# Queries and keys of a hybrid mixer as one token-stationary block with seven-product pairs, and all scores ahead of the values

## The chip, the cores and the metric

The kernel runs on one core of one Trainium2 chip. The metric is the device time of one execution in microseconds (us). Engines are named as in the profile: PE is TensorE (PEld its weight loads), DVE is VectorE, ACT is ScalarE, POOL is GpSimd, SP is the engine whose queue issues nearly all DMAs.

## What is computed

One layer of a streaming encoder on 256 tokens of width 2048, in f32: a half-step feed-forward, a mixer, cross attention to 256 memory tokens, a second half-step feed-forward, a final norm. The change lies in the mixer (and in the last units of the feed-forward ahead of it):

```python
h = rms_norm(x, mix_norm)
proj = h @ w_in        # 2048 x 4112: pool 1024 | q 512 | k 512 | v 1024 | gate 1024 | low-rank decay 16
u, q, k, v, g, a_lr = jnp.split(proj, list(IN_SPLITS), axis=-1)
y_pool = pool_mixer(u, pool_w, pool_scale)       # 4 groups: trailing means over 2, 4, 8, 16 tokens, then 256 x 256 each
y_gla = gla_mixer(q, k, v, g, a_lr, gla_w_a2, gla_b_a, gla_head_norm)
x = x + jnp.concatenate([y_pool, y_gla], axis=-1) @ w_out
...
# in gla_mixer: 4 heads, key width 128, value width 256, chunks of 64 tokens
log_a = jax.nn.log_sigmoid(a_lr @ w_a2 + b_a) / 16
cum = jnp.cumsum(chunks(log_a, GLA_DK), axis=2)
k_dec = kc * jnp.exp(cum[:, :, -1:] - cum)
scores = einsum(qc, k_dec)       # also from each chunk to the chunks before it, with the decays between
o = scores @ v                   # then a norm per head, and the product with silu(g)
```

## The kernel before

**Products.** Every large product is made of units of 1 MB of weights, [128, 2048] per unit. A weight is split into a high part wh (ScalarE, L1585) and a low part wl (VectorE, L453, `low_parts`), and an activation likewise (xs for the normed input, ys for a stage's inner result, each [128, 16, 2, 256]: k-tile, high or low, token). A product is high by high, high by low and low by high. There are three kinds of block:

- `block_a` (weights stationary): per k-tile and 128 output columns one matmul of 512 columns (high weight by high and low activation) and one of 256 (low weight by high activation). The result has channels on the partitions and comes in two halves, which `joined` adds (ScalarE copies one half out of PSUM, VectorE adds). A unit has 16 such pairs of matmuls, a block of 512 output columns has four units.
- `block_b` and `block_t` (tokens stationary, `products` at L362): 24 matmuls of 512 columns per unit. The result has tokens on the partitions.
- `block_s` (tokens stationary, 1024 output columns, 8 units, one per pair of k-tiles): for some pairs, the "sevens", the four 128 x 512 block products are replaced by seven products of sums (`seven`, L507): 21 matmuls instead of 24. Such a unit needs sums of activation blocks (`Sums.make`, made once, VectorE and ScalarE) and sums of weight blocks (`split_seven`: three sums into a tile T, the raw blocks' parts xh and xl, the sums' parts wh and wl). Its parts take all four PSUM buffers from the first seven until `combine` after the last one; `join` then adds them to the ordinary products, once for each half.

**Order.** `Stream` holds a list of units and of small operations; `st.op(f, n)` puts an operation n units later. `emit` splits a unit's weights two units ahead of its products, and issues the load of a unit three further. wh and wl have three buffers each, the raw weights three. `in_turn`, `among_weights` and `behind_weights` fix the place of an operation among the weight splits of VectorE and ScalarE. Within these bounds a planner, which simulates the engines' times while the program is built, settles the order on each engine: an instruction that it does not take for ready is moved behind others. A tile with n buffers waits until the tile n allocations before it under the same name has been read for the last time. `shared_tile` lets T, xh and xl stand in other tiles' buffers, by the "homes" given to the scope.

**PSUM** has four buffers of [128, 2, 512].

**The mixer** (L940 to L1225) before: a block_a for each half of the pool columns (`ev_pool`, L971: trailing sums in three "m4" buffers, result into ys 8 to 15); the unit of the 16 decay columns (`a_unit`, L1035); `decay` (L1052); a block_a for the queries and one for the keys (`ev_q`, `ev_k`), with channels on the partitions as the scores need them; the pool unit (`pool_unit`, L1003: 48 matmuls of 256 columns, reads ys 8 to 15, writes ys 0 to 7); two block_b for the values, and among them the scores of each head (`scores`, L1130, its decayed query tile in one m4 buffer, one score tile "ST" for all heads) and the outputs (`attend`, L1156); two block_a for the gate. The normed input's last k-tiles (`fold`, L785) are made after the mixer's first unit; the norm's row factors come from `finish_norm`, and `spread_norm` turns them into a row over all partitions by a small matmul.

Of the kernel before, what the change touches and what calls it, by code (L numbers as in the profile page):

```python
# [9 lines left out]
AF = mybir.ActivationFunctionType  # L10
ALU = mybir.AluOpType
# [3 lines left out]
P = 128  # L15
D = 2048
# [83 lines left out]
def build(ctx, tc, I, out):  # L100
# [303 lines left out]
    class Sums:  # L404
# [1 line left out]

        def __init__(self, name, act, pairs, over, room):
            self.name, self.act, self.pairs, self.over = name, act, pairs, over  # L410
            self.room, self.where = room, {}

        def make(self, g):
            act, i = self.act, self.pairs.index(g)
            n = 3 if self.over else 4
            if i == 0 or i >= self.room:
                room, tag = (self.room, self.name) if i == 0 else (1, f"{self.name}{i}")
                t = scope["pool"].tile([P, room * 6 * P], F32R, tag=tag, name=uid(tag))
                held = min(len(self.pairs), self.room) if i == 0 else 1
                t = t[:, : held * 2 * n * P].rearrange("p (g a n s) -> p g a n s", a=2, n=n, s=P)  # L420
                self.where.update({i + k: t[:, k] for k in range(held)})
            own = self.where[i]
            a, k = jtile(), slice(2 * g, 2 * g + 2)
            nc.vector.tensor_tensor(
                out=a.rearrange("p (k s) -> p k s", k=2), in0=f32(act[:, k, 0, :]),
                in1=f32(act[:, k, 1, :]), op=ALU.add,
            )

            a = a.rearrange("p (n s) -> p n s", n=4)
            p11, p21, p12, p22 = (a[:, m] for m in range(4))  # L430
            nc.vector.tensor_tensor(out=p11, in0=p11, in1=p21, op=ALU.subtract)
            nc.vector.tensor_tensor(out=p21, in0=p22, in1=p21, op=ALU.subtract)
            nc.vector.scalar_tensor_tensor(
                out=p22, in0=p11, scalar=-1.0, in1=p22, op0=ALU.mult, op1=ALU.subtract
            )
            added = nc.vector.tensor_tensor(out=p12, in0=p12, in1=p22, op=ALU.add)
            split(own[:, 0], own[:, 1], a[:, 4 - n :])
            if self.over:
                split(act[:, 2 * g, 0, P:], act[:, 2 * g, 1, P:], p11)
            return None, added  # L440
# [377 lines left out]
    REST = IntoX((0,), (2,), ((1, 2, 3, 4, 0, 5), None), ((0,), ()), False)  # L818
    END = IntoX((0,), None, None, None)

    def into_x(w, act, scale, gain=None, k0=0, nk=KT, spread_too=True, src=None, way=OUTPUT):

        for b in range(2):
            st.op(lambda b=b: fetch_x(b, src), 2)
            cols = wwide(w, b * 2 * NB, k0, nk)
            if way.sevens[b]:
                block_s(cols, act, way.sums, way.orders[b], residual(scale, b, 0),
                        early_parts(scale, b), way.sevens[b])
            else:
                block_t(cols, act, residual(scale, b))  # L830
            if gain is not None:
                for j in range(2):
                    st.op(lambda c=2 * b + j: fold(c, gain), way.folds[2 * b + j])
        if gain is not None:
            st.op(lambda: finish_norm(4, spread_too), way.folds[3] + 1)
            if spread_too:
                st.op(spread_norm, 3)

    FF_PARTS = ((0, 4), (4, 4), (8, 3))

# [88 lines left out]
    st.op(more_gains, 14)  # L929
    st.op(lambda: turn_gains(G_MIX, G_END), 35)  # L930

    def down_first(wd, k0, nk, last, way):
        way.make_sums()
        into_x(wd, ys, 0.5, G_MIX if last else None, k0, nk, src=None if k0 else I["x"][0],
               way=way)

    ffn(I["ffn1_w_gate"][0], I["ffn1_w_up"][0], I["ffn1_w_down"][0], down_first,
        amid_first)
    st.op(close_scope, 1)
    st.op(open_scope("s_mix"), 1)  # L940


    w_in = I["w_in"][0]
# [7 lines left out]
    def mixer_constants():  # L951
        keep = mt("keep", [P, S])
        nc.gpsimd.memset(keep, 1.0)
        for c in range(S // CH):
            nc.gpsimd.memset(keep[:, c * CH : c * CH + 1], 0.0)
        wa2 = mt("wa2", [32, H * DK])
        for i in range(2):
            nc.sync.dma_start(wa2[16 * i : 16 * i + 16, :], I["gla_w_a2"][0])

    st.op(mixer_constants, 2)  # L960

# [90 lines left out]
    def decay():  # L1052
        v = four(ptile(uid("pz")))
        for h in range(H):
            nc.tensor.matmul(
                v[:, h, :], mix["wa2"][:, h * DK : (h + 1) * DK], mix["aT"], start=True, stop=True
            )
        z, e, cum = (as_four(m4()) for _ in range(3))
        for h in range(H):
            nc.scalar.activation(z[:, h, :], v[:, h, :], AF.Identity, bias=gcol(G_BA + h))  # L1060
        nc.scalar.activation(e, z, AF.Abs)
        nc.scalar.activation(e, e, AF.Exp, scale=-1.0)
        nc.scalar.activation(e, e, AF.Ln, bias=1.0)
        nc.vector.scalar_tensor_tensor(
            out=z, in0=z, scalar=0.0, in1=e, op0=ALU.min, op1=ALU.subtract
        )
        for h in range(H):
            nc.vector.tensor_tensor_scan(
                out=cum[:, h, :], data0=mix["keep"], data1=z[:, h, :], initial=0.0,
                op0=ALU.mult, op1=ALU.add,  # L1070
            )
        ends = cum.rearrange("p h (c t) -> p (h c) t", t=CH)[:, :, CH - 1 : CH]
        E = mt("E", [P, 4 * 4])
        nc.scalar.activation(E, ends.rearrange("p a b -> p (a b)"), AF.Exp, scale=1.0 / 16)
        nc.vector.tensor_tensor(
            out=e.rearrange("p h (c t) -> p (h c) t", t=CH),
            in0=ends.to_broadcast([P, 16, CH]),
            in1=cum.rearrange("p h (c t) -> p (h c) t", t=CH), op=ALU.subtract,
        )
        nc.scalar.activation(e, e, AF.Exp, scale=1.0 / 16)  # L1080
        nc.gpsimd.tensor_tensor(out=e, in0=e, in1=bc(rows["R"], H), op=ALU.mult)
        mix["e"] = e

        Ev = E.rearrange("p (h c) -> p h c", c=4)
        F = mt("F", [P, 3, 4])
        nc.vector.tensor_tensor(out=F[:, 0, :], in0=Ev[:, :, 1], in1=Ev[:, :, 2], op=ALU.mult)
        nc.vector.tensor_tensor(out=F[:, 1, :], in0=Ev[:, :, 2], in1=Ev[:, :, 3], op=ALU.mult)
        nc.vector.tensor_tensor(out=F[:, 2, :], in0=F[:, 0, :], in1=Ev[:, :, 3], op=ALU.mult)

    def ev_q(p, ps):  # L1090
        if p == 0:
            mt("q", [P, H, S])
        q = mix["q"][:, 2 * p : 2 * p + 2, :]
        joined(ps, q)
        nc.vector.scalar_tensor_tensor(
            out=q, in0=q, scalar=DK ** -0.5, in1=bc(rows["R"]), op0=ALU.mult, op1=ALU.mult
        )

    def ev_k(p, ps):
        if p == 0:  # L1100
            mt("k", [P, H, S])
        k = mix["k"][:, 2 * p : 2 * p + 2, :]
        joined(ps, k)
        nc.vector.tensor_tensor(out=k, in0=k, in1=mix["e"][:, 2 * p : 2 * p + 2, :], op=ALU.mult)

    block_a(wblock(w_in, 0), xs, ev_pool(0))
    block_a(wblock(w_in, NB), xs, ev_pool(1))
    st.unit(load_a, a_unit, split_a)
    st.op(ev_a)
    st.op(decay, 2)  # L1110
    block_a(wblock(w_in, 2 * NB), xs, ev_q)
    block_a(wblock(w_in, 3 * NB), xs, ev_k)
    st.unit(load_pool, pool_unit)
    for g in range(4):
        st.op(lambda g=g: pool_out(g))

    def ev_v(b):
        def evict(ps):
            if b == 0:
                mt("v", [P, 2, 2 * NB])  # L1120
                s = mt("ST", [P, 2, S])
                nc.gpsimd.memset(s[64:128, 0, 0:CH], 0.0)
                nc.gpsimd.memset(s[64:128, 1, 2 * CH : 3 * CH], 0.0)
            for h in range(2):
                nc.scalar.activation(
                    mix["v"][:, h, b * NB : (b + 1) * NB], ps[:, h, :], AF.Copy, scale=Rcol[:, h : h + 1]
                )
        return evict

    def scores(h):  # L1130
# [14 lines left out]
        for j in range(4):  # L1145
# [2 lines left out]
            nc.tensor.matmul(  # L1148
                ps[part, j // 2, j * CH : S], kd[:, j * CH : (j + 1) * CH], rhs, start=True, stop=True
            )  # L1150
        s = mix["ST"]
        for j in range(4):
            part = slice((j % 2) * CH, (j % 2 + 1) * CH)
            nc.vector.tensor_copy(s[part, j // 2, j * CH :], ps[part, j // 2, j * CH : S])

    def attend(h):  # L1156
        s, v = mix["ST"], mix["v"]
        po = ptile(uid("po"))
        for vt in range(2):
            col = h * DV + vt * P  # L1160
# [38 lines left out]
    def ev_g(b):  # L1199
# [10 lines left out]
            split_pair(ys, 8 + 2 * h, t)  # L1210
        return evict

    for b in range(2):
        block_b(wblock(w_in, (4 + b) * NB), xs, ev_v(b))
        for i in range(2):
            h = 2 * b + i
            at = 1 + i - b
            st.op(lambda h=h: scores(h), at)
            st.op(lambda h=h: attend(h), at + 1)
            st.op(lambda h=h: head_squares(h), at + 1)  # L1220
        st.op(lambda b=b: head_norms(b), 5 - 2 * b)
        st.op(lambda b=b: head_scale(b), 6 - b)
# [404 lines left out]
```

## Time and profile before

| | us |
|---|---|
| median of 3 runs (2080.21 to 2080.56) | 2080.51 |
| the profiled execution | 2080.73 |
| its span, first to last instruction | 2078.8 |
| TensorE busy in it | 2066.5 |
| VectorE busy | 1811.7 |
| ScalarE busy | 1148.4 |
| GpSimd busy | 98.7 |

Matmuls are pipelined: one of 512 columns is shown with 390 ns, while the next starts about 227 ns later. The pace is therefore read from the chain of waits, where a row gives the time from one matmul's end to the next, or from the starts in order of time. In rows of the timeline and of groups, what stands behind the arrow in brackets or after the bar is what ended the engine's idle time before the instruction. "pa" are results of block_a, "pb" of block_b, "pt" of block_t and block_s, "px" and "ph" transposes, "pq" scores, "po" outputs, "pp" the pool unit, "pz" the decay's small product.

### The profile page before, as it was taken

How to read it: one execution, taken by the hardware profiler on the slowest of the kernel's cores; microseconds unless marked ns; L12 is line 12 of the kernel's file. 1: busy time of each engine (PE TensorE's matmuls, PEld its weight loads, DVE VectorE, ACT ScalarE, POOL GpSimd, SP SyncE). 2: the span in 40 equal slices, each digit the busy share in tenths (PEclk: the TensorE clock that was granted, in tenths of full speed). 3: DMA queues.
4: the chain of work that ended last, by engine and by line, in shares of the span. 5: the costliest groups of instructions: out<-in, count | busy, mean ns of one | idle time of the engine just before them, and what ended most of it. 6: DMA issues, size and time to landing. Idle time of an engine off the chain costs nothing.

```text
span 2078.8 us, 24366 instructions
## 1 busy us (share of the span) xinstructions
PE 2066.5 (99%) x9645; PEld 1724.5 (83%) x9645; DVE 1811.7 (87%) x1708; ACT 1148.4 (55%) x1144; POOL 98.7 (5%) x87
## 2 busy tenths in 40 slices
PE   9999999999999999999999999999999999999998
PEld 7888888888888888888888888888888888888886
DVE  7998899989998677579889878889988999889987
ACT  7655455644555545456756554566554555545554
POOL 0000000000000000000000000000000010000001
PEclk9999999999999999999999999999999999999999
DMA  7666666566656755556755455666576665676664
GB/s 264 204 202 223 242 219 215 187 227 228 235 194 220 248 178 182 163 181 225 264 183 194 169 182 182 203 213 216 179 243 217 235 209 190 224 241 222 211 225 152
DMA packets 131179, 435.95 MB, mean 210 GB/s; under 512 B 9844, under 2 KB 13528, under 8 KB 130680
## 3 DMA queue, kind: packets, MB, share of 16 engines
q1 hardware_dynamic: 130888, 433.86, 61.9%
q8 instruction: 76, 1.25, 0.2%
q10 hardware_dynamic: 176, 0.53, 0.1%
q14 instruction: 39, 0.32, 0.0%
HBM read 417.58 MB, written 16.78 MB: 209 GB/s over the span
## 4 chain that ended last, share of the span: by engine, by line
PE 99%; DMA 0%; DVE 0%; ACT 0%; SPq 0%; issue 0%; DVEq 0%; ACTq 0%
PE pt L362 58%; PE pt L507 28%; PE pa L347 7%; PE pb L362 2%; PE ph L780 1%; PE pl L1321 1%; PE pv L1358 1%; PE px L791 1%; DMA x<-in_x 0%; PE pp L1012 0%; PE pe L362 0%; PE pa L1039 0%; PE po L1161 0%; PE tm L1268 0%; PE px L717 0%; PE pq L1148 0%
## 5 line engine op out<-in xcount | busy, mean ns | idle before, releaser
L362 PE MATMUL pt<-wh,xs 128*128 128x512 f32 x2080 | 667.6, 390 | 0.2 <-ACT xs L236 0.2
L453 DVE TENSOR_TENSOR wl<-raw,wh 128x2048 fp32r<-128x2048 f32 (+1 forms) x251 | 540.1, 2159 | 121.3 <-ACT wh L1585 120.9
L1585 ACT CAST wh<-raw 128x2048 fp32r<-128x2048 f32 x251 | 479.3, 1913 | 266.6 <-PE pt L362 110.7
L489 ACT CAST wh<-T 128x1024 fp32r<-128x1024 f32 x246 | 258.4, 1054 | 374.8 <-DVE T L486 362.7
L362 PEld LDWEIGHTS pt<-wh,xs 128*128 128x128 f32 x2080 | 389.8, 188 | 80.3 <-ACT xs L236 0.4
L362 PE MATMUL pt<-wh,ys 128*128 128x512 f32 x1440 | 454.7, 389 | 0.0
L362 PE MATMUL pt<-wl,xs 128*128 128x512 f32 x1040 | 405.5, 391 | 0.0
L362 PEld LDWEIGHTS pt<-wh,ys 128*128 128x128 f32 x1440 | 270.2, 188 | 55.7
L362 PE MATMUL pt<-wl,ys 128*128 128x512 f32 x720 | 280.7, 390 | 0.0
L453 DVE TENSOR_TENSOR wl<-T,wh 128x2048 fp32r<-128x2048 f32 (+1 forms) x123 | 276.0, 2244 | 2.5 <-ACT wh L489 2.2
L362 PEld LDWEIGHTS pt<-wl,xs 128*128 128x128 f32 x1040 | 195.3, 188 | 39.9 <-DVE wl L280 0.2
L280 DVE TENSOR_TENSOR xl<-raw,xh 128x1536 fp32r<-128x1536 f32 x123 | 215.3, 1750 | 13.6 <-ACT xh L279 13.5
L279 ACT CAST xh<-raw 128x1536 fp32r<-128x1536 f32 x123 | 182.1, 1480 | 51.0 <-PE pt L507 32.3
L486 DVE TENSOR_TENSOR T<-T,raw 128x512 f32<-128x512 f32 x246 | 169.6, 690 | 6.4
L362 PEld LDWEIGHTS pt<-wl,ys 128*128 128x128 f32 x720 | 135.2, 188 | 28.2 <-DVE wl L453 0.3
L486 DVE TENSOR_TENSOR T<-raw 128x1024 f32<-128x1024 f32 x123 | 149.7, 1217 | 0.5
L507 PE MATMUL pt<-wh,xs 128*128 128x512 f32 x376 | 146.1, 389 | 0.0
L507 PE MATMUL pt<-xh,xs 128*128 128x512 f32 x376 | 140.3, 389 | 0.0
L457 POOL TENSOR_TENSOR wl<-raw,wh 128x768 fp32r<-128x768 f32 x40 | 74.3, 1857 | 1373.7 <-DVE wl L453 1293.4
L347 PE MATMUL pa<-xs,wh 128*128 128x512 f32 x384 | 135.6, 397 | 0.0
L507 PE MATMUL pt<-wh,xe 128*128 128x512 f32 x320 | 124.3, 389 | 0.0
L347 PE MATMUL pa<-xs,wl 128*128 128x256 f32 x384 | 106.8, 282 | 0.0
(248 smaller groups left out, 2374.3 us busy)
## 6 DMA issues: line engine op xcount, KB each, us to landing
raw<-in_ffn_w_down SPq DMA_DIRECT2D x88, 1024.0 KB, 5.6
raw<-in_ffn_w_up SPq DMA_DIRECT2D x80, 1024.0 KB, 5.0
raw<-in_ffn_w_gate SPq DMA_DIRECT2D x77, 1024.0 KB, 5.1
raw<-in_w_in SPq DMA_DIRECT2D x32, 1024.0 KB, 5.2
raw<-in_xattn_w_kv SPq DMA_DIRECT2D x32, 1024.0 KB, 5.0
raw<-in_w_out SPq DMA_DIRECT2D x16, 1024.0 KB, 5.6
raw<-in_xattn_w_q SPq DMA_DIRECT2D x16, 1024.0 KB, 5.7
raw<-in_xattn_w_o SPq DMA_DIRECT2D x16, 1024.0 KB, 5.9
```

The source lines that it names most:

```text
L279: in_turn("scalar", lambda: nc.scalar.copy(hi, src))
L280: in_turn("vector", lambda: nc.vector.tensor_tensor(out=lo, in0=src, in1=f32(hi), op=ALU.subtract))
L347: nc.tensor.matmul(o, w, x, start=k == 0 and i == 0, stop=last and i == 1)
L362: nc.tensor.matmul(ps, a, w, start=first and i == 0, stop=last and i == 2)
L453: in_turn("vector", lambda: nc.vector.tensor_tensor(out=lo[:, :n], in0=src[:, :n], in1=f32(hi[:, :n]), op=ALU.subtract))
L457: rest = nc.gpsimd.tensor_tensor(out=lo[:, n:], in0=src[:, n:], in1=f32(hi[:, n:]), op=ALU.subtract)
L486: in_turn("vector", lambda: nc.vector.tensor_tensor(out=o, in0=a, in1=b, op=ALU.add))
L489: in_turn("scalar", lambda: nc.scalar.copy(th[:, c], t[:, c]))
L507: nc.tensor.matmul(banks[n], x, w, start=n in fresh and j == 0, stop=n in ends and j == 2)
L780: nc.tensor.transpose(v[:, i, h * P : (h + 1) * P], g[:, h, i * P : (i + 1) * P], ident)
L791: nc.tensor.transpose(v[:, j, h * P : (h + 1) * P], x[:, h, j * P : (j + 1) * P], ident)
L1585: in_turn("scalar", lambda: nc.scalar.copy(hi, raw))
```

## The change

- Queries and keys (the 1024 columns from 1024 on) become one block_s of eight units, the first of the mixer, in the order of pairs 0, 2, 4, 1, 5, 3, 6, 7, with pairs 1 and 3 as sevens. The sums for these pairs are made in the last units of the down projection before, and stand in ys 12 to 15, which are free then (`in_ys`).
- The result has tokens on the partitions, is scaled there by the row factors (`ev_qk`), and is turned by 8 transposes for the keys and 8 for the queries (`turn_qk`). The decay now multiplies the keys on VectorE inside `decay`; GpSimd's product with the norm's row is gone.
- T stands in the buffer of the values "v", xh and xl have one buffer each (`MIX_HOMES`).
- After it come the decay unit, the two pool blocks, then the scores of heads 0 to 3 (after 0, 2, 4 and 6 units), with a score tile for each head; the pool unit moves behind the first half of the values.
- `spread_norm` comes 7 instead of 3 units after the down projection.

```diff
@@ -406,14 +406,14 @@
 
 
 
-        def __init__(self, name, act, pairs, over, room):
+        def __init__(self, name, act, pairs, over, room, where=None):
             self.name, self.act, self.pairs, self.over = name, act, pairs, over
-            self.room, self.where = room, {}
+            self.room, self.where, self.own = room, where or {}, where is None
 
         def make(self, g):
             act, i = self.act, self.pairs.index(g)
             n = 3 if self.over else 4
-            if i == 0 or i >= self.room:
+            if self.own and (i == 0 or i >= self.room):
                 room, tag = (self.room, self.name) if i == 0 else (1, f"{self.name}{i}")
                 t = scope["pool"].tile([P, room * 6 * P], F32R, tag=tag, name=uid(tag))
                 held = min(len(self.pairs), self.room) if i == 0 else 1
@@ -818,7 +818,8 @@
     REST = IntoX((0,), (2,), ((1, 2, 3, 4, 0, 5), None), ((0,), ()), False)
     END = IntoX((0,), None, None, None)
 
-    def into_x(w, act, scale, gain=None, k0=0, nk=KT, spread_too=True, src=None, way=OUTPUT):
+    def into_x(w, act, scale, gain=None, k0=0, nk=KT, spread_too=True, src=None, way=OUTPUT,
+               spread_at=3):
 
         for b in range(2):
             st.op(lambda b=b: fetch_x(b, src), 2)
@@ -834,7 +835,7 @@
         if gain is not None:
             st.op(lambda: finish_norm(4, spread_too), way.folds[3] + 1)
             if spread_too:
-                st.op(spread_norm, 3)
+                st.op(spread_norm, spread_at)
 
     FF_PARTS = ((0, 4), (4, 4), (8, 3))
 
@@ -929,15 +930,25 @@
     st.op(more_gains, 14)
     st.op(lambda: turn_gains(G_MIX, G_END), 35)
 
+    def in_ys(i):
+        t = ys[:, 2 * i : 2 * i + 2].rearrange("p k a s -> p (k a s)")
+        return t.rearrange("p (a n s) -> p a n s", a=2, n=4)
+
+    qk_sums = Sums("qe", xs, (1, 3), False, 2, {0: in_ys(6), 1: in_ys(7)})
+
     def down_first(wd, k0, nk, last, way):
         way.make_sums()
+        if last:
+            for g, after in zip(qk_sums.pairs, (9, 11)):
+                st.op(lambda g=g: among_weights(lambda: qk_sums.make(g)), after)
         into_x(wd, ys, 0.5, G_MIX if last else None, k0, nk, src=None if k0 else I["x"][0],
-               way=way)
+               way=way, spread_at=7)
 
     ffn(I["ffn1_w_gate"][0], I["ffn1_w_up"][0], I["ffn1_w_down"][0], down_first,
         amid_first)
     st.op(close_scope, 1)
-    st.op(open_scope("s_mix"), 1)
+    MIX_HOMES = {"T": [("v", D, 1)], "xh": [("xh", 3 * NB, 1)], "xl": [("xl", 3 * NB, 1)]}
+    st.op(open_scope("s_mix", MIX_HOMES), 1)
 
 
     w_in = I["w_in"][0]
@@ -956,6 +967,10 @@
         wa2 = mt("wa2", [32, H * DK])
         for i in range(2):
             nc.sync.dma_start(wa2[16 * i : 16 * i + 16, :], I["gla_w_a2"][0])
+        for h in range(H):
+            s = mix["ST", h] = mt("ST", [P, 2, S], bufs=H)
+            nc.gpsimd.memset(s[64:128, 0, 0:CH], 0.0)
+            nc.gpsimd.memset(s[64:128, 1, 2 * CH : 3 * CH], 0.0)
 
     st.op(mixer_constants, 2)
 
@@ -1078,8 +1093,7 @@
             in1=cum.rearrange("p h (c t) -> p (h c) t", t=CH), op=ALU.subtract,
         )
         nc.scalar.activation(e, e, AF.Exp, scale=1.0 / 16)
-        nc.gpsimd.tensor_tensor(out=e, in0=e, in1=bc(rows["R"], H), op=ALU.mult)
-        mix["e"] = e
+        nc.vector.tensor_tensor(out=mix["k"], in0=mix["k"], in1=e, op=ALU.mult)
 
         Ev = E.rearrange("p (h c) -> p h c", c=4)
         F = mt("F", [P, 3, 4])
@@ -1087,40 +1101,38 @@
         nc.vector.tensor_tensor(out=F[:, 1, :], in0=Ev[:, :, 2], in1=Ev[:, :, 3], op=ALU.mult)
         nc.vector.tensor_tensor(out=F[:, 2, :], in0=F[:, 0, :], in1=Ev[:, :, 3], op=ALU.mult)
 
-    def ev_q(p, ps):
-        if p == 0:
-            mt("q", [P, H, S])
-        q = mix["q"][:, 2 * p : 2 * p + 2, :]
-        joined(ps, q)
-        nc.vector.scalar_tensor_tensor(
-            out=q, in0=q, scalar=DK ** -0.5, in1=bc(rows["R"]), op0=ALU.mult, op1=ALU.mult
-        )
-
-    def ev_k(p, ps):
-        if p == 0:
-            mt("k", [P, H, S])
-        k = mix["k"][:, 2 * p : 2 * p + 2, :]
-        joined(ps, k)
-        nc.vector.tensor_tensor(out=k, in0=k, in1=mix["e"][:, 2 * p : 2 * p + 2, :], op=ALU.mult)
-
-    block_a(wblock(w_in, 0), xs, ev_pool(0))
-    block_a(wblock(w_in, NB), xs, ev_pool(1))
+    def query_rows():
+        mt("Rq", [P, 2])
+        nc.vector.tensor_scalar_mul(mix["Rq"], Rcol, DK ** -0.5)
+
+    def ev_qk(j, c):
+        for h in range(2):
+            nc.scalar.activation(
+                c[:, h, :], c[:, h, :], AF.Copy, scale=(Rcol if j else mix["Rq"])[:, h : h + 1]
+            )
+        mix["rows", j] = c
+
+    def turn_qk(j):
+        nc.scalar.copy(mt("k" if j else "q", [P, H, S]), rows_turned(mix["rows", j]))
+
+    def wide_home():
+        return mt("v", [P, 4, NB])
+
+    QK_ORDER = (0, 2, 4, 1, 5, 3, 6, 7)
+    st.op(query_rows, 3)
+    block_s(wwide(w_in, 2 * NB), xs, qk_sums, QK_ORDER, ev_qk, home=wide_home)
+    st.op(lambda: turn_qk(1), 1)
+    st.op(lambda: turn_qk(0), 2)
     st.unit(load_a, a_unit, split_a)
     st.op(ev_a)
     st.op(decay, 2)
-    block_a(wblock(w_in, 2 * NB), xs, ev_q)
-    block_a(wblock(w_in, 3 * NB), xs, ev_k)
-    st.unit(load_pool, pool_unit)
-    for g in range(4):
-        st.op(lambda g=g: pool_out(g))
+    block_a(wblock(w_in, 0), xs, ev_pool(0))
+    block_a(wblock(w_in, NB), xs, ev_pool(1))
 
     def ev_v(b):
         def evict(ps):
             if b == 0:
                 mt("v", [P, 2, 2 * NB])
-                s = mt("ST", [P, 2, S])
-                nc.gpsimd.memset(s[64:128, 0, 0:CH], 0.0)
-                nc.gpsimd.memset(s[64:128, 1, 2 * CH : 3 * CH], 0.0)
             for h in range(2):
                 nc.scalar.activation(
                     mix["v"][:, h, b * NB : (b + 1) * NB], ps[:, h, :], AF.Copy, scale=Rcol[:, h : h + 1]
@@ -1148,13 +1160,13 @@
             nc.tensor.matmul(
                 ps[part, j // 2, j * CH : S], kd[:, j * CH : (j + 1) * CH], rhs, start=True, stop=True
             )
-        s = mix["ST"]
+        s = mix["ST", h]
         for j in range(4):
             part = slice((j % 2) * CH, (j % 2 + 1) * CH)
             nc.vector.tensor_copy(s[part, j // 2, j * CH :], ps[part, j // 2, j * CH : S])
 
     def attend(h):
-        s, v = mix["ST"], mix["v"]
+        s, v = mix["ST", h], mix["v"]
         po = ptile(uid("po"))
         for vt in range(2):
             col = h * DV + vt * P
@@ -1210,12 +1222,17 @@
             split_pair(ys, 8 + 2 * h, t)
         return evict
 
+    for h, after in enumerate((0, 2, 4, 6)):
+        st.op(lambda h=h: scores(h), after)
     for b in range(2):
         block_b(wblock(w_in, (4 + b) * NB), xs, ev_v(b))
+        if b == 0:
+            st.unit(load_pool, pool_unit)
+            for g in range(4):
+                st.op(lambda g=g: pool_out(g))
         for i in range(2):
             h = 2 * b + i
             at = 1 + i - b
-            st.op(lambda h=h: scores(h), at)
             st.op(lambda h=h: attend(h), at + 1)
             st.op(lambda h=h: head_squares(h), at + 1)
         st.op(lambda b=b: head_norms(b), 5 - 2 * b)
```

## The prediction

> **What bounds the kernel now.** I read the page first, then who waited on TensorE, then the chain of waits through the mixer, then VectorE and ScalarE in order of time.
>
> ```profile
> span 2078.8 us, 24366 instructions
> PE 2066.5 (99%) x9645; PEld 1724.5 (83%) x9645; DVE 1811.7 (87%) x1708; ACT 1148.4 (55%) x1144; POOL 98.7 (5%) x87
> PEclk9999999999999999999999999999999999999999
> ...
> PE pwarm L206 <- POOL ident masks.py:199: 1.4, 1, 1.4
> PE px L717 <- DMA x<-in_x: 1.4, 1, 1.4
> PE pt L507 <- DVE xl L280: 0.2, 1, 0.2
> PE pt L362 <- ACT xs L236: 0.2, 1, 0.2
> ...
> 707.60:912.70 205.10, 205.10 (x1150) 176.60 (x1149) 140.63 (x192) 104.52 (x117) 3.80 (x11) 1.00 0.54 176
> ```
>
> TensorE waits 3.2 us in the whole span, 2.8 of it at the start. The last row is the mixer: its columns are length, then busy time of TensorE, its weight loads, VectorE, ScalarE and GpSimd, and the granted clock. TensorE is busy in all 205.1 us at clock 1.00; VectorE has 64 us free. There is no stall to win. The change can win only products, and can lose by a new wait of TensorE.
>
> **The products removed and added.** Rows of the chain: start, length, what, how many.
>
> ```profile
> 707.77 5.64 PE pa L347 x32
> 713.41 1.75 PE px L791 x16
> ...
> 726.70 28.23 PE pa L347 x160
> 754.94 3.65 PE pa L1039 x16
> ...
> 771.78 33.90 PE pa L347 x192
> 805.68 5.74 PE pp L1012 x48
> 811.42 27.23 PE pb L362 x120
> 838.65 0.79 PE pq L1148 x6
> ...
> 1140.92 1.75 PE ph L780 x16
> ...
> 1215.09 12.24 PE pt L507 x54
> ...
> 1387.99 31.32 PE pt L362 x138
> ```
>
> Queries and keys are two blocks of block_a: 8 units of 16 pairs (512 and 256 columns). 192 matmuls take 33.90 us, 0.1766 each, so 256 take 45.20 us. The new block has six ordinary units of 24 matmuls and two sevens of 21, so 186 of 512 columns. One costs 31.32/138 = 12.24/54 = 0.227 us: 42.20 us. Added are the two turns, 16 transposes with their seams: 1.75 us by the ph row. Sum: 42.20 + 1.75 - 45.20 = **-1.25 us**. The score and value matmuls, the pool unit and the gate unit only move; their count and seams stay.
>
> A sentence aside: the Trainium skill, page "TensorE: Matmul & The Clock Gate", Part 1, says that a warm matmul starts N/2.4 GHz plus about 2.5 ns after the one before, which would be 215.8, 109.2 and 55.8 ns at 512, 256 and 128 columns. By that rule, as an estimate, the sum is 40.1 + 0.9 - 41.6 = -0.6 us, half of mine. The trace does not agree for these types (227 ns at 512, 353 ns for a pair), and the rows decide.
>
> **VectorE and ScalarE ahead of the first seven.** A seven asks more of them than an ordinary unit, so its lead must be checked.
>
> ```profile
> L453 DVE TENSOR_TENSOR wl<-T,wh 128x2048 fp32r<-128x2048 f32 (+1 forms) x123 | 276.0, 2244 | 2.5 <-ACT wh L489 2.2
> L280 DVE TENSOR_TENSOR xl<-raw,xh 128x1536 fp32r<-128x1536 f32 x123 | 215.3, 1750 | 13.6 <-ACT xh L279 13.5
> L279 ACT CAST xh<-raw 128x1536 fp32r<-128x1536 f32 x123 | 182.1, 1480 | 51.0 <-PE pt L507 32.3
> L486 DVE TENSOR_TENSOR T<-T,raw 128x512 f32<-128x512 f32 x246 | 169.6, 690 | 6.4
> L486 DVE TENSOR_TENSOR T<-raw 128x1024 f32<-128x1024 f32 x123 | 149.7, 1217 | 0.5
> L489 ACT CAST wh<-T 128x1024 fp32r<-128x1024 f32 x246 | 258.4, 1054 | 374.8 <-DVE T L486 362.7
> ...
> 704.31 2.29 DVE L453 TENSOR_TENSOR wl<-raw,wh 128x2048 fp32r<-128x2048 f32 x1 [3.15 <-ACT wh L1585]
> 715.93 3.22 DVE L240 SCALAR_TENSOR_TENSOR xs<-px,gains,xs 128x256 fp32r<-128x256 f32 x8 [0.50 <-ACT xs L248]
> ```
>
> An ordinary unit takes 2.29 us of VectorE in 5.45 us of TensorE and leaves it 3.15 us idle, waiting for a weight buffer. A seven takes 1.22 + 2 x 0.69 + 1.75 + 2.24 = 6.59 us against 21 x 0.227 = 4.77 of TensorE. The first seven (fourth unit) is split in program order behind the third and fourth fold's low parts, which end at 715.93 + 3.22 = 719.15, now 0.2 earlier as the first unit is 5.45 instead of 5.64. So its sums run 718.95 to 721.55, the low part of the raw blocks ends at 723.30, that of the sums at 725.54 (the casts, 1.48 and 2 x 1.05 on ScalarE, lie between). TensorE reaches that unit at 707.77 + 5.45 + 1.75 + 2 x 5.45 = 725.87 and asks for the sums' low part in the fifth matmul at the latest, 0.9 later: 1.2 us in hand, against some 10 us for the unit there now. The cover is the three units before it; if it is gone, each us late is a us of TensorE.
>
> The second seven has only one buffer for its raw blocks ("xh", "xl") and so waits until the first has been multiplied: 725.87 + 4.77 - 0.68 (the last product doesn't read them) = 729.96. From there cast 1.48, low parts 1.75 and 2.24: 735.4. Queued behind the waiting instructions are the splits of the next two units, due at 740.9 and later. TensorE reaches the second seven at 730.64 + 5.45 = 736.1 and asks for the last of these 2.3 us later: 2.9 us in hand. I cost both at nothing; bounds 0 and 2 us together, since a late 2.29 us split ahead of either would eat one lead and a us more.
>
> Memory that the first seven's sums reuse from the stage before must be free: the store of x is issued at 709.06 and takes 5.8 us, to about 716, before 718.95.
>
> ```profile
> 709.06 0.81 SPq L752 DMA_DIRECT2D X<-x  x2
> X<-x SPq DMA_DIRECT2D x28, 512.0 KB, 5.8
> ```
>
> The queue of SP gets the same eight 1 MB loads, in wider rows; the gate's and the pool's loads keep their places among its waits or come later.
>
> **The rest beside the path.** The parts' combination, two joins, four scalings, two copies of the turned blocks and one product with the decay replace four evictions with two scalings of q, two products of k and a GpSimd product.
>
> ```profile
> L576 DVE TENSOR_TENSOR sg<-pt,sg 128x1024 f32<-128x1024 f32 x1 | 1.2, 1223 | 0.0
> L575 DVE TENSOR_TENSOR sg<-pt,sg 128x512 f32<-128x512 f32 x1 | 0.7, 691 | 0.0
> L1104 DVE TENSOR_TENSOR k<-k,m 128x512 f32<-128x512 f32 x2 | 1.4, 685 | 0.1
> L1125 ACT ACTIVATE v<-pb,Rcol 128x512 f32<-128x512 f32 x4 | 2.5, 685 | 8.1 <-PE pb L362 8.1
> L318 ACT COPY c<-pa 128x512 f32<-128x512 f32 x12 | 7.0, 582 | 16.1 <-PE pa L347 16.0
> ```
>
> VectorE: sevens 2 x (6.59 - 2.29) = 8.6, combination 1.22 + 2 x 0.69 = 2.6, joins 2.4, product 1.2, less eight of 0.69: 9.3 us more in a stage with 64 us free. ScalarE: 3.4 + 0.6 + 4 x 0.69 + two copies of 1.05 less four of 0.58: 6.5 us more of 100 free. Making the sums of pairs 1 and 3 (nearly 3 us of VectorE each) falls in the last units of the projection before, where VectorE idles 3.15 us of each unit. The turns: keys' rows are complete 12 matmuls (2.7 us) before the block ends, and join and scaling take 1.22 + 2 x 0.69 = 2.6; their transposes come a gate unit (3.65) later. The queries' turn comes a further 5.6 us later. The norm's row spread waits for PSUM that the seven parts hold from the fourth to the sixth unit, and now comes after the seventh; its reader is the gate's eviction after the ninth.
>
> **Scores and the pool unit.** Head 0's scores now come straight after the pool blocks, with no unit between. Their query tile is one of three "m4" buffers, all held there by the third pool group's sums.
>
> ```profile
> 754.28 0.59 ACT L318 COPY c<-pa 128x512 f32<-128x512 f32 x1 [3.11 <-PE pa L347]
> 754.90 0.69 DVE L319 TENSOR_TENSOR m<-pa,c 128x512 f32<-128x512 f32 x1 [1.41 <-ACT c L318]
> 764.07 0.67 DVE L990 SCALAR_TENSOR_TENSOR m<-m,m 128x512 f32<-128x512 f32 x1
> 775.56 0.69 DVE L286 TENSOR_TENSOR ys<-m,ys 128x512 fp32r<-128x512 f32 x1 [0.69 <-ACT ys L285]
> L1140 DVE TENSOR_SCALAR m<-q,E 128x64 f32<-128x64 f32 x12 | 2.7, 247 | 0.0
> ```
>
> The first buffer comes free at 764.74, 9.9 us after the block's last product (754.9); six factors of 0.17 apart add 1 us. If TensorE kept the written order it would stand still for 6.3 us (without the two weight splits that ran in between, 2 x 2.29) to 10.9 us. But the order on TensorE is made by a planner that moves what isn't ready: head 0's scores are now written after the first value unit, which ends at 811.42 + 24 x 0.227 = 816.9, and run at 838.65, four units later, with no idle time. I take nothing for it, and keep 6.3 to 10.9 for a rival. The pool unit now comes after four value units, 21.8 us; the four groups' sums took from 754.28 to 776.25, 22 us, and its fourth group is multiplied 4.3 us into the unit. That lead is some 4 us, from which the score copies take their share; bounds 0 and 3 us. Separate score tiles for the heads take away a wait of VectorE, not one of TensorE: nothing.
>
> **Sum.** The profiled execution took 2080.73 us, 1.9 us more than its span, and lies 0.2 us above the median of the runs (2080.51). 2080.73 - 1.25 = 2079.5 for it; from the median, **2079.3 us**.
>
> **The rivals.**
>
> 1. A seven comes late. For it: the lead falls to 1.2 us. Against it: the other stages run such sevens, four of eight units, and TensorE waited 0.2 us for them in the whole span. One to three us lost: 2080.3 to 2082.3.
> 2. Slower: head 0's scores hold TensorE behind the pool blocks. Price 6.3 to 10.9 us, 2085.6 to 2090.2, taken 2088. It decides if the planner takes the query tile for ready at the block's end. Against it speaks the delay to 838.65 now.
> 3. The pool unit comes late, or holds its weight buffers so that the next splits are: up to 3 us, 2082.3.
> 4. The change doesn't save what its products say: the seams of the turns and of products of other shapes eat it, 2080.5, plus or minus 0.4. Against it: 138 and 54 matmuls of both kinds run at one pace.
>
> **How the numbers follow.** Forecast 0.70; rivals 0.09, 0.10, 0.07 and 0.04. A measurement of this kernel can tell about 0.2% (4.2 us) from no change. Forecast, the first, the third and the fourth rival lie within it, all but a tail of 0.03: same 0.86, slower 0.13. Faster than 2076.3 would need three times the saving, for which there are no products: 0.01. The range from 2078.2 (the saving and the seams of the removed pairs, a further us) to 2083.0 holds all but the second rival and such tails.
>
> **What would show it.** Right: 186 new matmuls in about 42.2 us, two turns of 0.87 us, next to no wait of TensorE in the mixer, and head 0's scores some units behind the pool blocks. Wrong: TensorE idle at the first seven for its low parts, at the second for the raw blocks, or at the score matmuls for the query tile; or a span that shrank by over 4 us.

## The result, and the profile after

The changed kernel takes 2089.44 us (median of 6 runs, 2087.93 to 2089.89) against 2080.36 us before (6 runs): ratio 1.0043, 95% interval 1.003 to 1.0056. It is 0.43% slower. The forecast was 2079.3 us; the second rival, head 0's scores holding TensorE behind the pool blocks, had 2088 us and a tenth of the chance.

The page of the changed kernel, and who waited on TensorE in it (us in total, times, longest):

```profile
span 2088.1 us, 24282 instructions
PE 2069.6 (99%) x9591; PEld 1724.6 (83%) x9591; DVE 1822.2 (87%) x1727; ACT 1152.4 (55%) x1151; POOL 100.1 (5%) x94
...
PE pq L1160 <- DVE m L1152: 6.6, 1, 6.6
...
PE pt L507 <- DVE xl L280: 0.2, 1, 0.2
```

One wait is new, and it is a single one of 6.6 us: a score matmul waits for the query tile that ScalarE (L1150) and VectorE (L1152) make. The chain of waits through the mixer shows what stands before it:

```profile
713.46 1.75 PE px L791 x16
715.20 10.93 PE pt L362 x48
726.13 2.72 PE pt L507 x12
756.06 0.11 PE ph L780
...
756.87 0.76 PE ph L780 x7
...
762.49 0.87 PE ph L780 x8
...
770.83 33.40 PE pa L347 x188
...
804.25 0.60 ACT c L318
...
804.88 0.70 DVE m L319
...
807.04 2.29 DVE wl L453
809.32 0.64 DVE m L997
...
809.99 0.72 DVE m L997
...
810.73 0.17 DVE m L1001
810.91 0.50 DVE m L1152 x3
...
811.54 1.08 PE pq L1160 x2
812.63 5.99 PE pb L362 x18
818.62 0.58 PE pq L1160 x5
```

The pool blocks end (L347), and the third pool group's sums begin only then: its eviction on ScalarE and VectorE, its three trailing sums (L997) with a weight split of 2.29 us between them. When the third sum is done, one of the three m4 buffers is free, the query tile is written into it (L1150, L1152), and TensorE starts again. That it is the buffer that is waited for shows on ScalarE, whose copy of the long finished queries is released by the third sum:

```profile
810.79 0.54 ACT L1150 COPY m<-q 128x64 f32<-128x64 f32 x3 [3.42 <-DVE m L997]
```

Behind the waiting instruction stand 18 value products that need nothing of this: experiment 1 below runs them at once.

The wait costs more than its length. Rows of four stretches: length, busy time (and instructions) of TensorE, its weight loads, VectorE, ScalarE and GpSimd, then the granted clock of TensorE, the share and rate of the DMA engines.

```profile
805.00:809.00 4.00, 0.00 (x0) 0.00 (x0) 3.86 (x4) 2.37 (x2) 0.00 (x0) 1.00 0.73 231
809.40:811.50 2.10, 0.00 (x0) 0.00 (x0) 2.03 (x7) 0.54 (x3) 0.00 (x0) 0.50 0.42 87
811.50:816.00 4.50, 4.46 (x10) 3.06 (x11) 3.51 (x8) 0.62 (x1) 0.12 (x1) 0.50 0.51 197
816.30:820.00 3.70, 3.70 (x21) 2.78 (x20) 0.83 (x2) 0.00 (x0) 0.00 (x0) 1.00 0.00 0
```

TensorE's last product ended at 804.9. About 4.5 us into the idle time the clock is at a half, and it stays there until some 4.7 us after TensorE has begun again (811.54). The Trainium skill's page "TensorE: Matmul & The Clock Gate", Part 1, states that TensorE falls to half its clock after an idle window of about 3.4 us and needs a busy one to come back; the trace agrees in kind.

**Where 9 us went.** The stretch from the last folds (px) to the first product of the output projection can be read off the chain of every kernel, free of what differs at the program's start. The first product of the output projection, in the kernel before:

```profile
912.70 21.78 PE pt L362 x96
```

and in the changed kernel:

```profile
921.96 8.19 PE pt L362 x36
```

The folds start at 713.41 and 713.46, so the stretch is 199.29 us before and 208.50 us after: 9.21 more, of the spans' 9.3.

### The profile page after: what moved, and what is told of

Its sections match the earlier page's. It is cut to its first block, busy times and chain, and to the rows that moved or that the text cites. A ratio compares the mean times of both kernels' runs of the same rounds, so it can differ in the third digit from the quotient of the medians.

```text
span 2088.1 us, 24282 instructions
## 1 busy us (share of the span) xinstructions
PE 2069.6 (99%) x9591; PEld 1724.6 (83%) x9591; DVE 1822.2 (87%) x1727; ACT 1152.4 (55%) x1151; POOL 100.1 (5%) x94
## 4 chain that ended last, share of the span: by engine, by line
PE 98%; DVE 1%; DMA 0%; ACT 0%; issue 0%; SPq 0%; DVEq 0%; ACTq 0%
PE pt L362 59%; PE pt L507 28%; PE pa L347 4%; PE pb L362 2%; PE ph L780 1%; PE pl L1338 1%; PE pv L1375 1%; PE px L791 1%; DMA x<-in_x 0%; PE pp L1027 0%; PE pe L362 0%; DVE wl L453 0%; PE pq L1160 0%; PE pa L1054 0%; PE po L1173 0%; PE tm L1285 0%
## 5 line engine op out<-in xcount | busy, mean ns | idle before, releaser
L362 PE MATMUL pt<-wh,xs 128*128 128x512 f32 x2176 | 699.3, 391 | 0.0
L453 DVE TENSOR_TENSOR wl<-raw,wh 128x2048 fp32r<-128x2048 f32 (+1 forms) x249 | 534.0, 2152 | 117.0 <-ACT wh L1602 116.7
L362 PEld LDWEIGHTS pt<-wh,xs 128*128 128x128 f32 x2176 | 408.2, 188 | 83.7 <-ACT wh L1602 0.2
L362 PE MATMUL pt<-wh,ys 128*128 128x512 f32 x1440 | 455.1, 390 | 0.0
L362 PE MATMUL pt<-wl,xs 128*128 128x512 f32 x1088 | 424.8, 391 | 0.0
L362 PEld LDWEIGHTS pt<-wh,ys 128*128 128x128 f32 x1440 | 270.3, 188 | 55.6
L453 DVE TENSOR_TENSOR wl<-T,wh 128x2048 fp32r<-128x2048 f32 (+1 forms) x125 | 280.7, 2246 | 2.5 <-ACT wh L489 2.2
L362 PE MATMUL pt<-wl,ys 128*128 128x512 f32 x720 | 281.1, 391 | 0.0
L362 PEld LDWEIGHTS pt<-wl,xs 128*128 128x128 f32 x1088 | 204.6, 188 | 41.5
L362 PEld LDWEIGHTS pt<-wl,ys 128*128 128x128 f32 x720 | 135.2, 188 | 28.2 <-DVE wl L453 0.3
L507 PE MATMUL pt<-wh,xs 128*128 128x512 f32 x380 | 147.9, 390 | 0.0
L347 PE MATMUL pa<-xs,wh 128*128 128x512 f32 x256 | 90.7, 399 | 0.0
L507 PEld LDWEIGHTS pt<-xh,xs 128*128 128x128 f32 x384 | 72.1, 188 | 14.9
```

What stands on the lines that cost most here:

```text
L347: nc.tensor.matmul(o, w, x, start=k == 0 and i == 0, stop=last and i == 1)
L362: nc.tensor.matmul(ps, a, w, start=first and i == 0, stop=last and i == 2)
L453: in_turn("vector", lambda: nc.vector.tensor_tensor(out=lo[:, :n], in0=src[:, :n], in1=f32(hi[:, :n]), op=ALU.subtract))
L507: nc.tensor.matmul(banks[n], x, w, start=n in fresh and j == 0, stop=n in ends and j == 2)
```

## The experiments

Each is an edit of the changed kernel. "Stretch" is that from the last folds to the output projection in the profile.

**1. Query tiles in buffers of their own.** The two buffers of the sevens' raw parts are free at that time.

```diff
-        QD = m4()
+        QD = scope["pool"].tile([P, 3 * NB], F32, tag=("xh", "xl")[h % 2], name=uid("QD"), bufs=1)
```

> Changed kernel, but each head's decayed query tile stands in the buffers of the raw blocks' parts (free since the second seven) instead of one of the three m4 buffers. Order of the program unchanged: scores of head 0 still come straight behind the pool blocks. Theory A (the query tile waits for an m4 buffer that the third pool group's sums hold): TensorE's wait of 6.6 us at head 0's scores falls under 0.5 us, no half clock after it, 2079.3 us (2078.8 to 2080.0), 1.1 below before. Theory B (TensorE had nothing else to run there, as the value unit's weights or PSUM weren't ready): the wait moves to the first value product, 2085 or more. Theory C (the loss lies in the new block of sevens): 2088 or more.

Measured: 2079.22 us (11 runs) against 2080.17 (27 runs of the kernel before), ratio 0.9996, interval 0.9987 to 1.0005. The chain:

```profile
712.32 1.75 PE px L791 x16
...
794.96 8.81 PE pa L347 x50
803.77 0.79 PE pq L1160 x6
804.57 11.11 PE pb L362 x48
...
910.82 21.78 PE pt L362 x96
```

The scores still stand straight behind the pool blocks, and TensorE runs through them without a pause. The stretch is 198.50 us, 10.0 less than in the changed kernel and 0.8 less than before. So it was the m4 buffer (theory A). Theory C falls with it, as the block of sevens is in this kernel unchanged, and so does theory B, as the value products run at once.

**2. Head 0's scores one unit later**, buffers unchanged.

```diff
-    for h, after in enumerate((0, 2, 4, 6)):
+    for h, after in enumerate((1, 2, 4, 6)):
```

> Changed kernel, but head 0's scores due after one value unit instead of none (1, 2, 4, 6); buffers unchanged. Theory A with value products ready: TensorE runs value products in front and the wait is gone, 2079.3 us (2078.8 to 2080.0), if the planner puts the scores behind enough of them. Theory B: TensorE idles about 6 us before the first value product, 2086 to 2089. Theory C: 2088 or more.

Measured: 2081.06 us (11 runs), ratio 1.0005, interval 0.9996 to 1.0014: outside the range of theory A by 1.1 us, and far from B and C. The chain:

```profile
803.89 21.80 PE pb L362 x96
...
826.30 0.68 ACT v L1137
826.98 1.79 ACT wh L1602
828.76 0.15 ACT m L1150
...
828.96 0.65 PE pq L1160 x2
```

The planner put all four value units (96 products) ahead, though the scores were written behind the first. The 6.6 us are gone, which shows that the value products could have filled them. But three heads' scores now come together, and a later head's query tile waits on ScalarE, whose queue holds the values' eviction and a weight cast of 1.9 us: a new wait of 1.8 us.

**3. The scores at their old places, the rest of the change kept.**

```diff
-    for h, after in enumerate((0, 2, 4, 6)):
-        st.op(lambda h=h: scores(h), after)
...
+            st.op(lambda h=h: scores(h), at)
             st.op(lambda h=h: attend(h), at + 1)
```

> Changed kernel with the scores of each head back at their old places (among the values' second half), all else of the change kept (block of sevens, turned queries and keys, decay on the keys, four score tiles, pool unit behind the first half of the values). Theory A: no wait, 2079.3 us (2078.8 to 2080.2). Theory C: 2087 or more, since the block is still there.

Measured: 2078.78 us (10 runs, 2078.43 to 2079.18) against 2080.17, ratio 0.9993, interval 0.9984 to 1.0002. It has the lowest median of all, 1.4 us under before, and all its runs lie below all 27 of before (2079.66 to 2081.28), though the interval of the ratio holds 1. In the chain:

```profile
712.69 1.75 PE px L791 x16
...
910.91 21.78 PE pt L362 x96
```

The stretch is 198.22 us, 1.07 less than before. This is the change without its loss.

**4. Transposes in the wait**, to hold the clock: 44 of them, into a PSUM tile that nobody reads, ahead of head 0's scores.

```diff
+    st.op(lambda: spare_transposes(44))
     for h, after in enumerate((0, 2, 4, 6)):
```

> Changed kernel with 44 transposes into a PSUM tile that nobody reads, straight behind the pool blocks, ahead of head 0's scores: 4.8 us of work at the pace of 0.109 us inside the 6.6 us wait. Theory A with a clock that falls because TensorE stood idle: the scores start at the same time, the ten products behind them run at 227 instead of 427 ns, 2.3 us less than the changed kernel: 2087.1 us (2086.6 to 2087.6). If the slow products behind the wait come from something else (a transfer, the two kinds of matmul), the time stays 2089.4 or rises.

Measured: 2087.28 us (5 runs, 2086.13 to 2088.76) against 2080.17, ratio 1.0034, interval 1.0022 to 1.0047. The time lies where it was expected, but by luck: the profile doesn't show the reason that was expected, a whole clock behind the wait.

```profile
803.60 4.96 PE L206 MATMUL pwarm<-ident 128*128 128x128 f32 x44
810.39 0.62 PE L1160 MATMUL pq<-m,k 128*64 128x256 f32 x2 [1.82 <-DVE m L1152]
810.94 0.65 PE L362 MATMUL pb<-wh,xs 128*128 128x512 f32 x1
811.38 0.63 PE L362 MATMUL pb<-wl,xs 128*128 128x512 f32 x1
811.81 1.06 PE L362 MATMUL pb<-wh,xs 128*128 128x512 f32 x2
```

Two stretches of it, in the same columns as above:

```profile
808.50:810.30 1.80, 0.07 (x1) 0.00 (x0) 1.73 (x7) 0.54 (x3) 0.00 (x0) 1.00 0.45 72
811.20:814.50 3.30, 3.30 (x9) 2.56 (x9) 2.66 (x5) 0.30 (x1) 0.00 (x0) 0.50 0.48 186
```

TensorE was idle for 1.8 us only, and yet the next value products start about 430 ns after each other. The clock is still whole in the wait, and falls only when TensorE has begun again. That is some 7.4 us after the last ordinary product (803.8), against 4.5 us in the changed kernel. So the fall came later, and the time at half clock was shorter, but it was not none. The stretch (712.30 to 919.66) is 207.36 us, 1.1 less than in the changed kernel. The spans of the two profiled executions differ by 2.3 us, and the other 1.2 lie ahead of the folds (712.30 against 713.46), before the edit comes to bear. So "idle" was not the whole of it, which the next run took up.

**5. Products in the wait instead**, for as long.

```diff
+    def spare_products(n):
+        ps = ptile(uid("pwarm"))
+        for _ in range(n):
+            nc.tensor.matmul(
+                ps[:, 0, :], xs[:, 0, 0, :P], xs[:, 0].rearrange("p a b -> p (a b)"),
+                start=True, stop=True,
+            )
+
+    st.op(lambda: spare_products(21))
     for h, after in enumerate((0, 2, 4, 6)):
```

> Changed kernel with 21 matmuls of 512 columns on the products' own types, into a PSUM tile that nobody reads, straight behind the pool blocks: 4.8 us of products in the wait of 6.6 us, where the kernel with 44 transposes had 5.0 us of transposes and still ran its next eight products at half clock. Theory D (transposes don't count as work for the clock, products do): the wait that is left is 1.8 us, the clock stays whole, and the stretch from the last folds to the output projection is 2.3 us shorter than in the changed kernel, 206.2 instead of 208.5 us; in time about 2087.0. Theory E (any wait near 2 us behind the pool blocks drops it): eight to ten slow products as before, 207.4 to 208.5 us. The kernel with scores one unit later, whose wait of 1.8 us kept the clock, speaks for D.

Measured: 2086.45 us (6 runs, 2086.28 to 2087.52) against 2080.06, ratio 1.003, interval 1.0018 to 1.0041. The same columns of stretches as above:

```profile
803.50:808.50 5.00, 5.00 (x24) 4.06 (x22) 4.73 (x6) 2.85 (x3) 0.00 (x0) 1.00 0.65 207
808.50:810.60 2.10, 0.31 (x2) 0.00 (x0) 2.03 (x7) 0.54 (x3) 0.00 (x0) 1.00 0.36 78
810.60:815.00 4.40, 4.35 (x19) 3.35 (x20) 3.52 (x8) 0.62 (x1) 0.12 (x1) 1.00 0.53 204
```

The clock never leaves 1.00, with the same 1.8 us of wait left. In 810.6 to 815.0 TensorE runs 19 instructions; in the changed kernel's 811.5 to 816.0 it ran 10. The stretch (712.57 to 918.33) is 205.76 us, 2.7 less than in the changed kernel. Some 0.4 of that isn't the clock: head 1's scores take 0.80 us in one piece here, and 1.16 us in two pieces there. The half clock's price in the changed kernel is thus some 2.3 us, as expected. A whole clock behind this wait is what theory D expects and theory E does not. It rests on one trace of each kernel: the times of their runs overlap (2086.13 to 2088.76 with transposes, 2086.28 to 2087.52 with products).

**6. No sevens in the block**, on top of experiment 1: eight ordinary units; the sums for pairs 1 and 3 are made and not read. The new `ev_qt`, left out here, scales the result by the row factors on its way out of PSUM.

```diff
...
-    block_s(wwide(w_in, 2 * NB), xs, qk_sums, QK_ORDER, ev_qk, home=wide_home)
+    block_t(wwide(w_in, 2 * NB), xs, ev_qt)
```

> The kernel with the query tile in the raw parts' buffers, but the block of queries and keys with eight ordinary units and no seven (its sums for pairs 1 and 3 are still made, and not read). Six more products of 0.227 us: the stretch from the last folds to the output projection is 1.36 us longer, 199.9 against 198.5 us, time 2080.5. If the sevens' splits or their combination had a hidden cost on TensorE, the stretch grows by less, or shrinks.

Measured: 2080.86 us (10 runs) against 2080.06, ratio 1.0002, interval 0.9993 to 1.0012.

```profile
712.25 1.75 PE px L791 x16
...
912.15 21.78 PE pt L362 x96
```

The stretch is 199.90 us, 1.40 more than in experiment 1 and as expected: the six products saved cost what six products cost, and the sevens' splits cost TensorE nothing.

**7. Scores at their old places and query tiles in buffers of their own**: the edits of experiments 1 and 3 together.

> The kernel with the scores at their old places, and the query tiles in the raw parts' buffers besides. There the m4 buffers hold nothing back on TensorE, so the time should stay: 2078.8 us (2078.3 to 2079.4), stretch from the last folds to the output projection 198.2 us (197.9 to 198.5). A gain of more than 0.5 us would mean that an m4 wait was still hidden there.

Measured: 2079.40 us (11 runs, 2078.70 to 2080.51) against 2080.06, ratio 0.9996, interval 0.9987 to 1.0005; the stretch, 713.01 to 911.56, is 198.55 us. It isn't better than experiment 3, so at the old places no m4 wait was left to remove. The expectation was a little low in both numbers.

## Why the prediction was wrong

- **The step that failed** is in the part on the scores: "head 0's scores are now written after the first value unit, which ends at [...] 816.9, and run at 838.65, four units later". They were written after the fifth. The operations are handed to the stream behind `block_b`, when its four units already stand in the list, so their delays count from the block's end: four units and one more are 120 products, and the quoted row "811.42 27.23 PE pb L362 x120" ends exactly where the scores begin. TensorE had kept the written order. What I took for proof that the planner moves unready work was no move at all. On it rested the term that failed, "I take nothing for it", where the runs showed 10.0 us (6.6 of wait and what hangs on it), and the weight of 0.10 for the second rival.
- **The rival's mechanism** was right as worked out: the place, the buffers, the price of 6.3 to 10.9 us (6.6 measured, with one of the two weight splits in it, and the buffer freed by the third sum rather than by the last reader of the first buffer). Its time of 2088 us came within 1.4 us of the measured 2089.44, in part by luck: the 6.6 us measured, on top of the forecast, give 2085.9, and the half clock and the cut scores, which make most of the rest, were left out. Against experiment 1, the 10.0 us are: 6.6 of wait; 1.8 for the first eight value products (3.58 us from 812.56 to 816.14 where eight take 1.82); 0.9 and 0.4 for the scores of heads 0 and 1, which the planner had cut in two (1.66 and 1.16 us against 0.79, part of the first at half clock); some 0.3 in small seams.
- **Does the planner move work?** Yes, as experiment 2 shows (96 products ahead instead of 24). Why it left two score matmuls in front here and moved the others behind 18 value products is open: its own times for VectorE aren't in a trace.
- **The products** were right: -1.25 us forecast, -1.07 in experiment 3 and -0.79 in experiment 1, the difference lying in seams where scores cut into the values. The stretch begins behind the mixer's first unit, and so leaves out some 0.2 us of the forecast's saving (5.45 against 5.64 us for that unit). The six products of the sevens alone are 1.40 us by experiment 6, where 1.36 was expected.
- **The lead of the first seven** was right nearly to the tenth. VectorE in order of time in the changed kernel:

```profile
719.12 1.21 DVE L486 TENSOR_TENSOR T<-raw 128x1024 f32<-128x1024 f32 x1
...
723.37 2.28 DVE L453 TENSOR_TENSOR wl<-T,wh 128x2048 fp32r<-128x2048 f32 x1
...
730.36 1.75 DVE L280 TENSOR_TENSOR xl<-raw,xh 128x1536 fp32r<-128x1536 f32 x1
732.08 2.29 DVE L453 TENSOR_TENSOR wl<-T,wh 128x2048 fp32r<-128x2048 f32 x1
```

The first seven's last low part ends at 725.65 (725.54 forecast), and TensorE comes to it at 726.13. The second's ends at 734.4, an us ahead of the forecast. Neither is waited for, and the first and the third rival did not come true. The turns take 0.87 us each (rows of ph above, 0.11 + 0.76 for the keys).
- **What would show it** named the right place: TensorE idle "at the score matmuls for the query tile".

## What to carry to other kernels

Before a trace is taken as proof that a scheduler moves work, count from the code where that work was written: a delay counts from the place of the call, and products counted along the chain give the place to the instruction. When an operation loses the units between it and its inputs, look for the buffer that its first write needs, not only for the data; the cure was to take a buffer that was idle anyway. A long wait of TensorE should be priced with the half clock behind it: here the clock fell some 4.5 us into the wait, and cost some 2.3 us on top of 6.6.

## What the runs showed of the hardware

In the profiled execution, transposes did not hold the clock: 44 of 128 columns over 5.0 us, then 1.8 us idle, were followed by eight products at half clock, while 21 products over 4.9 us and the same 1.8 us left it whole. With the transposes the fall came later than with an idle TensorE, some 7.4 against 4.5 us after the last ordinary product, so they were not quite without effect. A wait of 1.8 us within ordinary products (experiment 2) didn't drop the clock either (1.00 from 829 to 833, behind it). The Trainium skill's page "TensorE: Matmul & The Clock Gate", Part 4, says in a remark that transposes don't count as busy in the same way; the pair of runs agrees with it, though these are f32 transposes, and other f32 matmuls were not tried. Each kernel was profiled once, and whether the fall depends on when the wait comes was not tested.
